# Building the gate tables of a product-key expert layer: bf16 key compares for eight tokens, gates applied by ScalarE

## The chip, the cores and the metric

One core of one Trainium2 chip runs the whole program. The metric is the device time of one execution in microseconds (us). The kernel before takes 3887.56 us, the median of three runs from 3883.04 to 3895.33.

## The reference, cut to what matters

The program is one decoder block on 1024 tokens of 1024 features. Its first part (RWKV-7 time mixing, sparse attention, a merge and a LayerNorm) is not touched here. The change lies in the last part, a layer of 128 x 128 single-neuron experts that are chosen by two keys of 128 values each:

```
s = einsum('thcd,hcnd->thcn', (h @ w_pq) as (token, 8 heads, 2 halves, 64), sub_keys)
s1, i1 = top_k(s[:, :, 0], 16);  s2, i2 = top_k(s[:, :, 1], 16)
top_s, pos = top_k(all sums s1 + s2, 16)           # per token and head
experts = i1 * 128 + i2 at pos                     # 8 heads * 16 = 128 slots per token
gates   = softmax(top_s)
act = gelu(sum_d h[t, d] * u[experts]) * gates;    y[t] = sum over slots act * v[experts]
```

## The kernel before, in words

The 1024 tokens are eight tiles of 128. Tiles 0 to 2 are served by gathering: for each of their 768 rows of experts, GpSimd issues an indirect DMA (L1375) that fetches 128 rows of u or v, and VectorE multiplies and sums them (L1379 for u, L1383 for v). Tiles 3 to 7 (640 tokens) are served densely: all 16384 experts are multiplied with all 640 tokens on TensorE, and a table of gates, zero for an expert that a token did not choose, masks the result. That table `gtD`, token by i1 by i2, is what the change is about.

`retrieve` (one tile) finds the keys: TensorE scores them (L1131), VectorE takes the best sixteen (L1140 to L1148, four steps of two heads each), forms the sums and turns positions into keys and gates (L1154 to L1220). `by_slot` transposes a tile's i1, i2 and gates so that the 128 slots lie on the partitions and the 128 tokens along the free axis (`slots`). `gate_table` then makes the tile's table in 16 blocks of 8 tokens. For each token it needs two matrices of 128 slots x 128 keys: a one-hot matrix of i2 (all eight tokens in one VectorE instruction, L1251), and a one-hot matrix of i1 whose ones are replaced by the slot's gate. The second is made per token: for six tokens of the eight (`ONE_HOT`) by VectorE in fp32, for the other two by a pair of ScalarE instructions:

```
V.tensor_scalar(oh[:, 8 + t], iotan, slots[:, 0, c], slots[:, 2, c], op0=OP.is_equal, op1=OP.mult)   # L1256
A.activation(oh[:, 8 + t], iota, AF.Square, bias=slots[:, 0, c])                                      # L1258
A.activation(oh[:, 8 + t], oh[:, 8 + t], AF.Relu, scale=ng[:, c], bias=slots[:, 2, c])                # L1259
```

TensorE multiplies the two (L1263, one fp32 product per token, which the trace shows as two matmul records), four tokens to a bank of PSUM `tp`, and ScalarE copies each bank (the helper `copy`, L233) into `st`, where the token is the innermost index. Every four blocks `st` goes to `gtD` by DMA (L1267). `gt` has two buffers, `tp` two banks, `st` two halves.

The tables run in a stage of their own, together with other work that the program's scheduler interleaves into one fixed order per engine: 60 of 69 `dots` (a product of a 128-expert slice of u with all 640 tokens: a 512 KB load, ScalarE's split `whi` at L233, GpSimd's `wlo` at L1276, 48 matmuls at L1289 to L1293, and ScalarE's copy `ds`), some 150 rows of the gather, and the retrieval of the next tile. Four times, a tile's table is followed by the end of the next tile's retrieval; tile 7's table comes last and alone. Then the dense stage begins (L1289 to L1293 on u and v, with the rest of the gather beside it).

Of the kernel before, what the change touches and what calls it, by code (L numbers as in the profile page):

```python
# [28 lines left out]
AB = 12  # L29
LAG = 4  # L30
EARLY = 128
ONE_HOT = 6
M1 = 3
J0 = 4
JF = 0
# [16 lines left out]
TD = NG * 128  # L52
# [151 lines left out]
def body(tc, a, out, dbg=None, ntiles=8, mark=lambda s: None):  # L204
# [4 lines left out]
    base = pool("base")  # L209
# [14 lines left out]
    def ptp(dt=F32):  # L224
        return banks[0].tile([128, 512], dt, name="tp", bufs=2)
# [5 lines left out]
    mm = nc.tensor.matmul  # L231
    V, A, G = nc.vector, nc.scalar, nc.gpsimd
    copy = lambda o, i, **k: A.activation(o, i, AF.Copy, **k)  # L233
# [106 lines left out]
        at, n = RW[name]  # L340
        nc.sync.dma_start(dst, a["rows"][0:1, at:at + n].to_broadcast([parts, n]))

    ident, iota, iotan = (base.tile([128, 128], F32, name=n) for n in ("ident", "iota", "iotan"))
# [12 lines left out]
    def constants():  # L356
# [15 lines left out]
        V.tensor_scalar(iotan, iota, -1.0, None, op0=OP.mult)  # L372

        rowb(gnx.rearrange("p a b -> p (a b)"), "gng", 8)
        V.tensor_tensor(gnx, gnx, spread(), op=OP.mult)
# [859 lines left out]
    def by_slot(found, dst):  # L1235

        i1, i2, gates = found
        tp = ptp()
        for n, src in enumerate((i1, i2, gates)):
            nc.tensor.transpose(tp[:, n * 128:(n + 1) * 128], src, ident)  # L1240
        copy(dst[:, 0, :], tp[:, 0:128], scale=-1.0)
        copy(dst[:, 1:3, :].rearrange("p a b -> p (a b)"), tp[:, 128:384])


    def gate_table(i, slots, sl, du, st):
        ng = sl.tile([128, 128], F32, name="ng")
        V.tensor_scalar(ng, slots[:, 2, :], -1.0, None, op0=OP.mult)
        for b in range(max(0, TD - i * 128) // 8, 16):
            s_ = st[:, b // 4 % 2]
            oh = du.tile([128, 16, 128], F32, name="gt", bufs=2)  # L1250
            V.tensor_tensor(oh[:, 0:8], iota[:, None, :].to_broadcast([128, 8, 128]),  # L1251
                            slots[:, 1, b * 8:b * 8 + 8, None].to_broadcast([128, 8, 128]), op=OP.is_equal)
            for t in range(8):
                c = slice(b * 8 + t, b * 8 + t + 1)
                if t < ONE_HOT:
                    V.tensor_scalar(oh[:, 8 + t], iotan, slots[:, 0, c], slots[:, 2, c], op0=OP.is_equal, op1=OP.mult)  # L1256
                else:
                    A.activation(oh[:, 8 + t], iota, AF.Square, bias=slots[:, 0, c])  # L1258
                    A.activation(oh[:, 8 + t], oh[:, 8 + t], AF.Relu, scale=ng[:, c], bias=slots[:, 2, c])  # L1259
            for u in range(2):  # L1260
                tp = ptp()
# [189 lines left out]
    slots = {}  # L1451
# [151 lines left out]
    with tc.tile_pool(reuse_waits=REUSE, name="du", bufs=1) as du, \  # L1603
# [6 lines left out]
        with tc.tile_pool(reuse_waits=REUSE, name="slots", bufs=1) as sl, \  # L1610
                tc.tile_pool(reuse_waits=REUSE, name="ps2", bufs=2, space=PSUM) as banks[0]:
            st = sl.tile([128, 2, 128, 32], F32, name="st")
            found = {}

            def table(i, f=None):
                if f:
                    by_slots(i, f)
                found[i] = gate_table(i, slots[i], sl, du, st)

            for i in slots:  # L1620
                table(i)
# [72 lines left out]
```

## Time and profile before

| | |
|---|---|
| median of three runs | 3887.56 us |
| the profiled execution, its time / its span | 3895.0 / 3893.1 us |
| TensorE (PE) busy in the span | 3552.1 us, 91% |
| VectorE (DVE) busy | 2761.7 us, 71% |
| ScalarE (ACT) busy | 1611.3 us, 41% |
| GpSimd (POOL) busy | 1989.5 us, 51% |
| the stage of the tables | from 1791 to 2504 us of the span |

The shares are averages over stages with different limits: the stage of the tables is read by itself, in windows of the span, by groups of instructions and in order of time. A busy time of a group is the time covered by its instructions; the mean is of single instructions, which overlap a little where they follow each other. L233 is the one line of all ScalarE copies, so those are told apart by the tiles they read and write. The clock is the share of full speed that TensorE was granted.

### The profile page before, as it was taken

Reading aid. Unit: us, or ns where it says so; the run is one execution under the profiler, and the core shown is the slowest. Engines: PE = TensorE matmul, PEld = TensorE weight load, DVE = VectorE, ACT = ScalarE, POOL = GpSimd, SP = SyncE. Lnnn points to the kernel's source line nnn. Section 1 sums busy time; section 2 is a strip of 40 time slices with the busy share of each in tenths; the row PEclk is TensorE's granted clock in tenths of the full one; section 3 lists DMA queues with packets and bytes.
Section 4 is the critical chain, followed back from the end, with each engine's and each line's share of the span. In section 5 each row is a group of like instructions: output and inputs, shape, how many; then the busy total and the mean of one; then the engine's idle time right before and its main releaser. Section 6 shows DMA issues by size and latency. Waiting matters only on the chain.

```text
span 3893.1 us, 65065 instructions
## 1 busy us (share of the span) xinstructions
PE 3552.1 (91%) x24045; PEld 3174.2 (82%) x24045; DVE 2761.7 (71%) x5983; ACT 1611.3 (41%) x2909; POOL 1989.5 (51%) x1566
## 2 busy tenths in 40 slices
PE   8698999888989999688999888899999999999997
PEld 7476777666677777578888888799999999999996
DVE  7556653848377766959999999666776766666753
ACT  3448953243345443425464554632222322222222
POOL 5242222255455553245445454167676666776765
PEclk9899999889999999789999999999999999999998
DMA  6463323864666666277777777589998998898973
GB/s 228 125 189 96 104 90 113 289 198 156 216 216 221 208 219 198 96 259 262 248 259 240 261 262 270 213 315 328 327 329 323 322 329 323 320 334 315 330 255 114
DMA packets 438170, 924.63 MB, mean 238 GB/s; under 512 B 36596, under 2 KB 198588, under 8 KB 434908
## 3 DMA queue, kind: packets, MB, share of 16 engines
q1 hardware_dynamic: 315132, 502.04, 38.6%
q0 software_dynamic: 122720, 418.43, 30.6%
q8 instruction: 190, 3.11, 0.3%
q14 instruction: 128, 1.05, 0.1%
HBM read 792.64 MB, written 127.68 MB: 236 GB/s over the span
## 4 chain that ended last, share of the span: by engine, by line
PE 41%; DVE 20%; DMA 16%; POOL 9%; issue 8%; ACT 4%; SPq 1%; POOLq 0%; ACTq 0%; DVEq 0%
PE pair L1289 5%; PE pair L1291 5%; PE pair L1293 5%; PE acc L429 4%; PE acc L430 4%; PE acc L431 4%; POOL g L1375 4%; POOL wlo L1276 4%; DMA g<-in_v_dram,gidx 3%; DMA raw<-in_ut_dram 3%; DVE pg L1383 3%; DVE gt L1256 3%; DMA g<-in_u_dram,gidx 3%; DMA raw<-in_vt_dram 2%; DVE g L1379 2%
## 5 line engine op out<-in xcount | busy, mean ns | idle before, releaser
L1276 POOL TENSOR_TENSOR wlo<-raw,whi 128x1024 fp32r<-128x1024 f32 x264 | 640.5, 2427 | 304.7 <-ACT whi L233 299.9
L419 POOL TENSOR_TENSOR wlo<-wraw,whi 128x512 fp32r<-128x512 f32 x280 | 374.0, 1338 | 598.8 <-ACT whi L233 530.5
L1383 DVE SCALAR_TENSOR_TENSOR pg<-g,dots,pg 128x1024 f32<-128x1024 f32 x381 | 488.5, 1282 | 154.1 <-DMA g<-in_v_dram,gidx 140.4
L1375 POOL DMA_INDIRECT g<-in_u_dram,gidx x384 | 403.6, 1051 | 354.7 <-DVE g L1379 208.0
L1375 POOL DMA_INDIRECT g<-in_v_dram,gidx x384 | 384.8, 1002 | 368.6 <-DVE pg L1383 167.4
L233 ACT ACTIVATE whi<-raw 128x1024 fp32r<-128x1024 f32 x264 | 278.6, 1056 | 710.0 <-PE pair L1291 366.4
L1289 PE MATMUL pair<-A,whi 128*128 128x320 f32 (+2 forms) x2048 | 482.4, 312 | 25.8 <-DVE A L1321 20.3
L1289 PE MATMUL pair<-h2T,whi 128*128 128x320 f32 x2048 | 478.8, 314 | 14.0 <-DMA h2T<-h2TD 11.1
L1291 PE MATMUL pair<-h2T,whi 128*128 128x320 f32 x2048 | 481.6, 314 | 3.6 <-DMA h2T<-h2TD 3.6
L1291 PE MATMUL pair<-A,whi 128*128 128x320 f32 (+2 forms) x2048 | 481.5, 311 | 2.2 <-DVE A L1321 1.6
L1293 PE MATMUL pair<-A,wlo 128*128 128x320 f32 (+2 forms) x2048 | 480.2, 311 | 2.5 <-POOL wlo L1276 2.5
L1293 PE MATMUL pair<-h2T,wlo 128*128 128x320 f32 x2048 | 480.2, 314 | 0.3 <-POOL wlo L1276 0.3
L429 PE MATMUL acc<-big,whi 128*128 128x512 f32 x864 | 359.8, 417 | 52.3 <-ACT whi L233 18.2
L1379 DVE SCALAR_TENSOR_TENSOR g<-g,pg 128x1024 f32<-128x1024 f32 x256 | 308.8, 1215 | 118.8 <-DMA g<-in_u_dram,gidx 116.4
L1289 PEld LDWEIGHTS pair<-A,whi 128*128 128x128 f32 x2048 | 348.8, 190 | 28.9 <-issue 20.1
L1289 PEld LDWEIGHTS pair<-h2T,whi 128*128 128x128 f32 x2048 | 348.7, 191 | 15.4 <-issue 11.3
L431 PE MATMUL acc<-big,wlo 128*128 128x512 f32 x864 | 353.7, 410 | 2.8 <-POOL wlo L419 2.5
L430 PE MATMUL acc<-big,whi 128*128 128x512 f32 x864 | 352.0, 407 | 3.7 <-DVE big L455 3.7
L1291 PEld LDWEIGHTS pair<-h2T,whi 128*128 128x128 f32 x2048 | 349.2, 191 | 5.4 <-DMA h2T<-h2TD 3.9
L1291 PEld LDWEIGHTS pair<-A,whi 128*128 128x128 f32 x2048 | 349.2, 190 | 3.8 <-DVE A L1321 2.8
L1293 PEld LDWEIGHTS pair<-A,wlo 128*128 128x128 f32 x2048 | 348.7, 190 | 3.0 <-POOL wlo L1276 3.0
L1293 PEld LDWEIGHTS pair<-h2T,wlo 128*128 128x128 f32 x2048 | 348.2, 191 | 2.0 <-POOL wlo L1276 0.5
(483 smaller groups left out, 6632.6 us busy)
## 6 DMA issues: line engine op xcount, KB each, us to landing
raw<-in_vt_dram SPq DMA_DIRECT2D x136, 512.0 KB
raw<-in_ut_dram SPq DMA_DIRECT2D x128, 512.0 KB
gtD<-st SPq DMA_DIRECT2D x20, 2048.0 KB
gt<-gtD SPq DMA_DIRECT2D x32, 1280.0 KB
wraw<-in_wz_dram SPq DMA_DIRECT2D x152, 256.0 KB
dotD<-ds SPq DMA_DIRECT2D x69, 320.0 KB
al<-dotD SPq DMA_DIRECT2D x69, 320.0 KB
mw<-in_wada_dram SPq DMA_DIRECT2D x32, 512.0 KB
```

Source lines behind the costliest of these rows:

```text
L233: copy = lambda o, i, **k: A.activation(o, i, AF.Copy, **k)
L419: G.tensor_tensor(lo, raw, hi.bitcast(F32), op=OP.subtract)
L429: mm(pt, lhsT=wh[:, ks], rhs=ah[:, k, :], start=k == 0, stop=False)
L430: mm(pt, lhsT=wh[:, ks], rhs=al[:, k, :], start=False, stop=False)
L431: ins = mm(pt, lhsT=wl[:, ks], rhs=ah[:, k, :], start=False, stop=k == nk - 1)
L1276: G.tensor_tensor(lo, raw, hi.bitcast(F32), op=OP.subtract)
L1289: mm(pts[n], lhsT=wh, rhs=ah[:, h], start=k == 0, stop=False)
L1291: mm(pts[n], lhsT=wh, rhs=al[:, h], start=False, stop=False)
L1293: mm(pts[n], lhsT=wl, rhs=ah[:, h], start=False, stop=last)
L1375: G.indirect_dma_start(out=u, out_offset=None, in_=a["u" if n < 2 else "v"], in_offset=bass.IndirectOffsetOnAxis(ap=idx[:, k:k + 1], axis=0))
L1379: V.scalar_tensor_tensor(u, u, 1.0, h2, op0=OP.mult, op1=OP.mult, accum_out=dots[:, k:k + 1])
L1383: V.scalar_tensor_tensor(acc, u, dots[:, k:k + 1], acc, op0=OP.mult, op1=OP.add)
```

## The change

`by_slot` now writes i1 as bf16 (128 keys are exact in it) into the third plane of `slots`, and no longer negated. A new constant `keys8` holds each key eight times in a row in bf16, made once by a ScalarE copy. For a block of 8 tokens, one VectorE instruction compares `keys8` with the block's eight first keys and writes a bf16 one-hot `hot`, slot by key by token. Eight ScalarE copies then take token t's column out of it, read with a step of eight elements, and put the gate in as the scale of the copy. So L1256, L1258, L1259 and the constants `iotan` and `ng` go. TensorE's products are the same, but are written to PSUM with the token innermost, so that neighbouring results of one product lie four words apart; ScalarE's copy to `st` then reads PSUM in order and writes runs of four tokens. `gt` grows from 16 to 20 units of 128 words, which is the room that the dense stage's `gt` has anyway.

```diff
-        for n, src in enumerate((i1, i2, gates)):
+        for n, src in enumerate((i2, gates, i1)):
             nc.tensor.transpose(tp[:, n * 128:(n + 1) * 128], src, ident)
-        copy(dst[:, 0, :], tp[:, 0:128], scale=-1.0)
-        copy(dst[:, 1:3, :].rearrange("p a b -> p (a b)"), tp[:, 128:384])
+        copy(dst[:, 0:2, :].rearrange("p a b -> p (a b)"), tp[:, 0:256])
+        copy(first_keys(dst), tp[:, 256:384])
+    first_keys = lambda slots: slots[:, 2, 0:64].bitcast(BF)
...
+            room = du.tile([128, 20, 128], F32, name="gt", bufs=2)
+            oh2, oh1 = room[:, 0:8], room[:, 8:16]
+            hot = room[:, 16:20].rearrange("p a b -> p (a b)").bitcast(BF).rearrange("p (a b) -> p a b", b=8)
+            V.tensor_tensor(hot, keys8, k1[:, None, b * 8:b * 8 + 8].to_broadcast([128, 128, 8]), op=OP.is_equal)
...
             for t in range(8):
-                c = slice(b * 8 + t, b * 8 + t + 1)
-                if t < ONE_HOT:
-                    V.tensor_scalar(oh[:, 8 + t], iotan, slots[:, 0, c], slots[:, 2, c], op0=OP.is_equal, op1=OP.mult)
-                else:
-                    A.activation(oh[:, 8 + t], iota, AF.Square, bias=slots[:, 0, c])
-                    A.activation(oh[:, 8 + t], oh[:, 8 + t], AF.Relu, scale=ng[:, c], bias=slots[:, 2, c])
+                copy(oh1[:, t], hot[:, :, t], scale=slots[:, 1, b * 8 + t:b * 8 + t + 1])
...
-                    mm(tp[:, t * 128:(t + 1) * 128], lhsT=oh[:, 4 * u + t], rhs=oh[:, 8 + 4 * u + t], start=True, stop=True)
+                    mm(tp[:, :, t], lhsT=oh2[:, 4 * u + t], rhs=oh1[:, 4 * u + t], start=True, stop=True)
...
-                copy(s_[:, :, t0:t0 + 4].rearrange("p a b -> p b a"), tp.rearrange("p (b a) -> p b a", b=4))
+                copy(s_[:, :, t0:t0 + 4], tp)
...
+            keys8 = sl.tile([128, 128, 8], BF, name="keys8")
+            copy(keys8, iota[:, :, None].to_broadcast([128, 128, 8]))
```

The scheduler makes a new order for the stage; before it and after it every engine's order is what it was. VectorE near the start of tile 4's table, before (L1383 are rows of the gather, L1140 the next tile's sort):

```order
L1251 TENSOR_TENSOR gt<-iota,slots 128x1024
L1256 TENSOR_SCALAR gt<-iotan,slots 128x128 x6
L1383 SCALAR_TENSOR_TENSOR pg<-g,dots,pg 128x1024
L1251 TENSOR_TENSOR gt<-iota,slots 128x1024
L1256 TENSOR_SCALAR gt<-iotan,slots 128x128 x6
L1383 SCALAR_TENSOR_TENSOR pg<-g,dots,pg 128x1024
L1140 MAX v_16603<-sc 128x8 x4
```

The same place now (L1254 is the bf16 compare, L1255 the compare of second keys, L1138 the sort):

```order
L1254 TENSOR_TENSOR gt<-keys_15601,slots 128x1024
L1255 TENSOR_TENSOR gt<-iota,slots 128x1024
L1383 SCALAR_TENSOR_TENSOR pg<-g,dots,pg 128x1024 x3
L1254 TENSOR_TENSOR gt<-keys_15601,slots 128x1024
L1255 TENSOR_TENSOR gt<-iota,slots 128x1024
L1383 SCALAR_TENSOR_TENSOR pg<-g,dots,pg 128x1024 x2
L1138 MAX v_16580<-sc 128x8 x2
```

Seven instructions per block have become two, and two or three rows of the gather stand between blocks where one stood. Over the four tables that have other work beside them, rows of the gather between a table's first and last block go from 78 to 106 (all in all some 150 stand in the stage in both), all four steps of the next tile's sort stand inside the table where one of them stood behind it, and on TensorE 38.8 `dots` are issued inside those tables where 30.8 were (21.6 between the tables, where 29.5 were).

ScalarE in the last table, before and then now (L233 and L232 are the helper `copy`):

```order
L1258 ACTIVATE gt<-iota,slots 128x128 x2
L1259 ACTIVATE gt<-gt,slots,ng 128x128 x2
L233 ACTIVATE st<-tp 128x4x128 x2
L1258 ACTIVATE gt<-iota,slots 128x128 x2
L1259 ACTIVATE gt<-gt,slots,ng 128x128 x2
```

```order
L232 ACTIVATE gt<-gt,slots 128x128 x8
L232 ACTIVATE st<-tp 128x128x4 x2
L232 ACTIVATE gt<-gt,slots 128x128 x8
L232 ACTIVATE st<-tp 128x128x4 x2
L232 ACTIVATE gt<-gt,slots 128x128 x8
```

Four small instructions per block have become eight, and the two copies out of PSUM walk it in another order. No dot and no row of the gather stands beside the last table, before or now.

## Rows read from the trace of the kernel before

**Rows 1.** Windows: the first four tables, the last table, most of the dense stage.
```profile
core 0: us, PE busy (x) PEld busy (x) DVE busy (x) ACT busy (x) POOL busy (x), PEclk, DMA share, GB/s
1791.00:2451.00 660.00, 594.25 (x4081) 577.06 (x4080) 646.78 (x1637) 341.63 (x568) 318.22 (x208) 0.96 0.75 257
2451.00:2504.00 53.00, 36.69 (x257) 33.70 (x257) 45.76 (x112) 50.13 (x94) 3.26 (x1) 0.90 0.33 136
2600.00:3700.00 1100.00, 1078.47 (x7282) 1074.79 (x7281) 765.26 (x937) 301.09 (x368) 758.34 (x569) 0.99 0.90 325
```

**Rows 2.** Waits between 1791 and 2451: who waited, total, times, longest (us).
```profile
ACT st L233 <- PE tp L1263: 116.1, 52, 8.4
POOL g L1375 <- DVE pg L1383: 85.7, 42, 5.0
...
PE tp L1263 <- DVE gt L1256: 35.1, 19, 3.9
```

**Rows 3.** Groups of VectorE's instructions between 1791 and 2451: busy us, mean ns, idle.
```profile
L1256 DVE TENSOR_SCALAR gt<-iotan,slots 128x128 f32<-128x128 f32 x384 | 162.5, 488 | 0.0
L1383 DVE SCALAR_TENSOR_TENSOR pg<-g,dots,pg 128x1024 f32<-128x1024 f32 x105 | 133.9, 1275 | 6.0 <-DMA g<-in_v_dram,gidx 5.8
L1251 DVE TENSOR_TENSOR gt<-iota,slots 128x1024 f32<-128x1024 f32 x65 | 86.0, 1323 | 0.0
...
L1146 DVE FIND_INDEX8 i<-v,sc 128x8 uint32<-128x128 f32 x64 | 17.9, 280 | 0.0
```

**Rows 4.** All engines in order of time in the last table: one block.
```profile
2466.19 1.95 ACT L233 ACTIVATE st<-tp 128x512 f32<-128x512 f32 x2
...
2467.29 2.07 PE L1263 MATMUL tp<-gt 128*128 128x128 f32 x16 [1.00 <-ACT st L233]
2467.53 1.62 DVE L1256 TENSOR_SCALAR gt<-iotan,slots 128x128 f32<-128x128 f32 x6
2467.92 0.67 ACT L1258 ACTIVATE gt<-iota,slots 128x128 f32<-128x128 f32 x2
...
2468.47 0.87 ACT L1259 ACTIVATE gt<-gt,slots,ng 128x128 f32<-128x128 f32 x2
2469.24 1.95 ACT L233 ACTIVATE st<-tp 128x512 f32<-128x512 f32 x2
```

**Rows 5.** VectorE, then GpSimd, in order of time in tile 4's table: start, length.
```profile
1957.64 3.71 DVE L1256 TENSOR_SCALAR gt<-iotan,slots 128x128 f32<-128x128 f32 x6
...
1956.69 3.30 POOL L1276 TENSOR_TENSOR wlo<-raw,whi 128x1024 fp32r<-128x1024 f32 x1 [0.83 <-ACT whi L233]
```

**Rows 6.** Single lines: instructions, duration in ns as min/median/max, first and last start.
```profile
L1188 DVE TENSOR_TENSOR ge<-wx,ranks x32: 626/692/1233, 918.6 to 2438.8; 128x1024 bf16<-128x1024 bf16 x32
...
L1251 DVE TENSOR_TENSOR gt<-iota,slots x80: 1192/1210/3242, 1791.0 to 2496.9; 128x1024 f32<-128x1024 f32 x80
...
L1196 DVE TENSOR_TENSOR wp<-wp x24: 405/424/2784, 1909.8 to 2442.3; 128x512 bf16<-128x512 bf16 x24
```

**Rows 7.** Windows, sums: the four tables with other work, then the four stretches between.
```profile
sum 403.00, PE 369.49 PEld 355.37 DVE 397.36 ACT 258.33 POOL 181.01; mean PE 92.37 PEld 88.84 DVE 99.34 ACT 64.58 POOL 45.25
...
sum 254.00, PE 222.76 PEld 219.69 DVE 246.42 ACT 82.27 POOL 135.78; mean PE 55.69 PEld 54.92 DVE 61.61 ACT 20.57 POOL 33.94
```

**Rows 8.** Groups of ScalarE's instructions by shape, whole span.
```profile
L233 ACT ACTIVATE st<-tp 128x512 f32<-128x512 f32 x160 | 165.5, 1110 | 119.2 <-PE tp L1263 118.8
...
L1258 ACT ACTIVATE gt<-iota,slots 128x128 f32<-128x128 f32 x160 | 52.6, 386 | 0.0
...
L233 ACT ACTIVATE pT<-tp 128x512 f32<-128x512 f32 x48 | 28.4, 593 | 24.6 <-PE tp L975 24.4
...
L233 ACT ACTIVATE p<-p,asm 128x128 f32<-128x128 f32 x8 | 3.2, 398 | 0.0
```

**Rows 9.** The chain that ended last, pieces in order of time: a block's products; a gather.
```profile
2020.95 1.78 PE tp L1263 x16
...
2139.17 9.79 DMA g<-in_v_dram,gidx
```

More of the change, by code (lines that the diff above doesn't have):

```diff
@@ L31 @@
 EARLY = 128
-ONE_HOT = 6
 M1 = 3
@@ L341, in rowb @@
         nc.sync.dma_start(dst, a["rows"][0:1, at:at + n].to_broadcast([parts, n]))
-    ident, iota, iotan = (base.tile([128, 128], F32, name=n) for n in ("ident", "iota", "iotan"))
+    ident, iota = (base.tile([128, 128], F32, name=n) for n in ("ident", "iota"))
     ranks = base.tile([128, 3, 16], BF, name="ranks")
@@ L371, in constants @@
         nc.sync.dma_start(iota, a["more"][:, 1152:1280])
-        V.tensor_scalar(iotan, iota, -1.0, None, op0=OP.mult)
         rowb(gnx.rearrange("p a b -> p (a b)"), "gng", 8)
@@ L1238, in by_slot @@
         tp = ptp()
-        for n, src in enumerate((i1, i2, gates)):
+        for n, src in enumerate((i2, gates, i1)):
             nc.tensor.transpose(tp[:, n * 128:(n + 1) * 128], src, ident)
-        copy(dst[:, 0, :], tp[:, 0:128], scale=-1.0)
-        copy(dst[:, 1:3, :].rearrange("p a b -> p (a b)"), tp[:, 128:384])
[L1245 to L1248, printed above, removed]
-            s_ = st[:, b // 4 % 2]
-            oh = du.tile([128, 16, 128], F32, name="gt", bufs=2)
-            V.tensor_tensor(oh[:, 0:8], iota[:, None, :].to_broadcast([128, 8, 128]),
-                            slots[:, 1, b * 8:b * 8 + 8, None].to_broadcast([128, 8, 128]), op=OP.is_equal)
-            for t in range(8):
-                c = slice(b * 8 + t, b * 8 + t + 1)
-                if t < ONE_HOT:
-                    V.tensor_scalar(oh[:, 8 + t], iotan, slots[:, 0, c], slots[:, 2, c], op0=OP.is_equal, op1=OP.mult)
-                else:
-                    A.activation(oh[:, 8 + t], iota, AF.Square, bias=slots[:, 0, c])
-                    A.activation(oh[:, 8 + t], oh[:, 8 + t], AF.Relu, scale=ng[:, c], bias=slots[:, 2, c])
@@ new lines, in by_slot, with gate_table @@
+        copy(dst[:, 0:2, :].rearrange("p a b -> p (a b)"), tp[:, 0:256])
+        copy(first_keys(dst), tp[:, 256:384])
+    first_keys = lambda slots: slots[:, 2, 0:64].bitcast(BF)
+    def gate_table(i, slots, sl, du, st, keys8):
+        k1 = first_keys(slots)
+        for b in range(16):
+            s_ = st[:, b // 4 % 2]
+            room = du.tile([128, 20, 128], F32, name="gt", bufs=2)
+            oh2, oh1 = room[:, 0:8], room[:, 8:16]
+            hot = room[:, 16:20].rearrange("p a b -> p (a b)").bitcast(BF).rearrange("p (a b) -> p a b", b=8)
+            V.tensor_tensor(hot, keys8, k1[:, None, b * 8:b * 8 + 8].to_broadcast([128, 128, 8]), op=OP.is_equal)
+            V.tensor_tensor(oh2, iota[:, None, :].to_broadcast([128, 8, 128]),
+                            slots[:, 0, b * 8:b * 8 + 8, None].to_broadcast([128, 8, 128]), op=OP.is_equal)
+            for t in range(8):
+                copy(oh1[:, t], hot[:, :, t], scale=slots[:, 1, b * 8 + t:b * 8 + t + 1])
@@ L1260, in gate_table @@
             for u in range(2):
-                tp = ptp()
+                tp = ptp().rearrange("p (a b) -> p a b", b=4)
                 for t in range(4):
-                    mm(tp[:, t * 128:(t + 1) * 128], lhsT=oh[:, 4 * u + t], rhs=oh[:, 8 + 4 * u + t], start=True, stop=True)
+                    mm(tp[:, :, t], lhsT=oh2[:, 4 * u + t], rhs=oh1[:, 4 * u + t], start=True, stop=True)
                 t0 = b % 4 * 8 + 4 * u
-                copy(s_[:, :, t0:t0 + 4].rearrange("p a b -> p b a"), tp.rearrange("p (b a) -> p b a", b=4))
+                copy(s_[:, :, t0:t0 + 4], tp)
@@ L1617, in table @@
                     by_slots(i, f)
-                found[i] = gate_table(i, slots[i], sl, du, st)
+                found[i] = gate_table(i, slots[i], sl, du, st, keys8)
             for i in slots:
```

## The prediction

> **What bounds the kernel now.** I read the windows of the stage first, then who waits for whom, then the costliest groups on the fullest engine, and last the order of time in one block. The change touches nothing outside 1791 to 2504 us, so only this stage is priced. In its first 660 us VectorE is busy 646.8 us, 98%, and TensorE 594.3 us, 90%; in the dense stage behind it TensorE is at 1078.5 of 1100 us, 98%, and VectorE has room [rows 1]. So VectorE sets the pace of the first four tables. The waits agree: GpSimd's gathers wait for VectorE to free a buffer, and TensorE's products for the gates that VectorE writes; what ScalarE waits for most is those products [rows 2]. The group that costs VectorE most is L1256, the six fp32 instructions per block that this change removes: 162.5 us [rows 3].
>
> Part of that is not work. Six of them take 1.62 us undisturbed [rows 4], so the 64 blocks hold 64 x 1.62 = 104 us of work; the other 59 us are spent as where the six take 3.71 us while GpSimd's `wlo` runs [rows 5].
>
> In the last table (2451 to 2504 us) the pace is another engine's: ScalarE is busy 50.1 of 53 us [rows 1]. It takes 2469.24 - 2466.19 = 3.05 us per block, and TensorE waits 1 us per block for its copy out of PSUM [rows 4]. Here a faster VectorE buys nothing, and any time added on ScalarE is paid in full.
>
> **VectorE's part.** Out go L1256's 162.5 us. In come 64 bf16 compares of 128x1024. The nearest row is L1188, the same compare of a bf16 tile of that size with a short row repeated along it: 0.69 us [rows 6], so 64 x 0.69 = 44 us. They can meet `wlo` too: L1251 beside them pays 1323 - 1210 = 0.11 us for it on the mean [rows 3, 6], which makes 51 us, and L1196, a bf16 instruction, has met it for up to 2.8 us [rows 6]. The bounds are thus 51 us and 44 + 59 = 103 us (all of L1256's waiting stays); VectorE sheds 111 us or 60 us. I take 111, since half of the instructions that could wait are gone. L1251 itself is unchanged.
>
> **What the stage then takes.** VectorE falls from 647 to 536 us (587 at worst), below TensorE's 594. TensorE's work is the same, so it becomes the limit, but not everywhere, because the new order moves work. A dot is 48 matmuls at 1078.5 / 7282 = 0.148 us [rows 1], 7.1 us. Eight dots more inside the tables, eight fewer between:
> - tables: TensorE 369.5 + 57 = 426 us; VectorE 397.4 + 28 gather rows x 1.28 [rows 3] + four sort steps of twenty instructions at 0.28 (22) - 111 = 344 us [rows 7] (395 at worst);
> - between: TensorE 222.8 - 57 = 166 us; VectorE 246.4 - 27 x 1.28 - 22 = 190 us.
>
> The longer ones are 426 + 190 = 616 us; at the dense stage's 98% that is 628 us. [...] I take 620: **-40 us** (bounds: 603 with no loss, -57; 646 if TensorE reaches 94% in the tables, -14). What is late next is then a product of TensorE's, and VectorE begins to wait for `gt` buffers.
>
> **ScalarE's part.** Per block the four small instructions (0.67 + 0.87 us [rows 4], less overlap) become eight copies with a scale per partition. The row is `p<-p,asm`, such a copy of 128x128: 398 ns alone [rows 8]. Two L1258 of 386 ns take 0.67, so in a run each hides 0.10 us: 0.30 us per copy, 2.4 us for eight. No row shows what it costs to read every eighth element. The upper bound is the copy `st<-tp`, which writes with a long step: 1110 ns against 593 for `pT<-tp`, the same 512 elements written in order [rows 8], 1.0 ns more per element, 0.13 per copy: 0.43, 3.4 us for eight. The two copies to `st` now write four words in a row; between 0.49 us each (as `pT`, less overlap) and today's 0.95. The block is thus 3.4 to 5.3 us. I take 3.75 (0.33 and 0.55): the row with a price has its step on the write, and that step has become runs of four. For the last table: 16 x (3.75 - 3.05) = **+11 us** (bounds +6 and +36). In the first four tables ScalarE has the cover: it is busy 258 of 403 us [rows 7].
>
> [...]
>
> **At nothing:** `keys8` is one ScalarE copy ahead of the first table, while VectorE is still at the retrieval; `by_slot` keeps two copies, `ng` and `iotan` are two small VectorE instructions. SP issues the same loads and stores, GpSimd the same gathers and `wlo`; the same bytes in 620 us are a DMA share of 0.75 x 660 / 620 = 0.80, and the dense stage runs at 0.90 [rows 1]. If that cover failed, a gather that arrives late costs up to 9.8 us at a time on the chain [rows 9].
>
> **Sum:** -40 + 11 = -29 us on the profiled execution's 3895.0: 3866. That execution is 7.4 us above the median of 3887.56, so on the median I predict **3858**. The dense stage's order is the same, and it starts when the last table is written, so the gain is kept.
>
> **Rivals.**
> *A, slower: the products' new place in PSUM.* Each product now writes results four words apart. No row shows a matmul that does so. If it costs what a stepped write costs ScalarE, a factor 1110 / 593 = 1.87 [rows 8], a block's products rise from 1.78 [rows 9] by 1.55 us; 64 blocks add 99 us to TensorE in the tables: (426 + 99 + 190) / 0.98 = 730, +70, and with the last table's +11 the time is 3887.6 + 81 = 3969. It decides from about 0.45 us per block (25%), where the 29 us are used up. Against it: a product needs 1.78 / 8 = 0.22 us for 128 results per partition, 1.7 ns each, while the dots write one in 0.148 / 320 = 0.46 ns, so the write side has room. 18%. [...]
> *B: ScalarE becomes the limit.* At 5.3 us per block it needs 85 us a table, and some 20 for the dots and scores, 105 of TensorE's 106. An engine that works in order and waits for products will not fill that: 115 us a table, 460 + 194 = 654, -6, and +36 at the end: 3918. For it, ScalarE's many waits for products [rows 2]; against it, that needs both upper bounds at once. 8%.
> *C: the time does not come free.* Both engines are now loaded alike and tied by two buffers; TensorE has 92% of the table windows today [rows 7]. At 94% the first four tables give -14, with the last table's +11 that is -3: 3885. 17%.
>
> **Chances.** The forecast with its neighbours (3830 to 3875) has 57%. A measurement of this kernel can tell about 0.3%, 12 us, from no change. Faster takes the forecast and a little of C: 0.60; same most of C and the mild ends of A and B: 0.17; slower the rest of A and B: 0.23. The range reaches from the gain with no loss (-57 + 6, 3836, and a few us for the clock, 3830) to B's end, 3918; most of A lies outside. The forecast's own range is 3830 to 3875.
>
> **What the profile after would show.** Right: the compare near 0.7 us, TensorE above 94% and VectorE under 92% between 1791 and the last table, that stretch near 620 us, the last table near 64 us with ScalarE full. A shows as products of a block over 2.2 us, B as ScalarE copies over 0.4 us and ScalarE over 90% in the tables, C as waits of TensorE for ScalarE's or VectorE's `gt` that replace those for L1256. Wrong altogether if the first four tables stay at 660 us although L1256 is gone.

## The result, and the profile after

The changed kernel takes 3912.65 us (median of 20 runs, 3893.93 to 3922.2) against 3887.62 us of the kernel before (20 runs): a ratio of 1.0059, 95% interval 1.0047 to 1.0071. It is slower by 25 us; the prediction was 3858, faster. The profiled execution took 3913.4 us, with a span of 3911.6 against 3893.1 before.

The windows of the changed kernel: the first four tables (1787 to 2439), the last (2439 to 2514), most of the dense stage.

```profile
1787.00:2439.00 652.00, 593.91 (x4073) 578.43 (x4073) 533.08 (x1314) 408.06 (x826) 311.48 (x210) 0.95 0.75 261
2439.00:2514.00 75.00, 47.11 (x286) 43.33 (x285) 29.11 (x32) 70.31 (x163) 2.35 (x1) 0.80 0.23 97
2600.00:3700.00 1100.00, 1072.48 (x7227) 1069.62 (x7226) 762.68 (x941) 301.46 (x369) 753.43 (x566) 0.99 0.90 324
```

Against [rows 1], VectorE's share in the first four tables fell from 98% to 533.08 / 652 = 82%, but TensorE's only rose from 90% to 91%: no engine fills the stretch any more, and the stretch is hardly shorter. Measured from the first table's first compare of second keys to the last table's first, the four take 651.9 us against 659.8, and the last, from there to the start of its last eviction (ScalarE's copy out of a bank of PSUM into `st`), 74.2 against 52.1. These two measures, "four" and "last", stand in the table below for every run. The stage is 14 us longer in the profiled execution. The rest of the span's 18.5 us lies behind it (1398.4 us from the stage's end on, against 1390.2) and ahead (it starts 4 us earlier). In the profiled executions that follow the part behind lies between 1384.6 and 1411.6 us without an order that fits the edits, so I do not read a cause into it.

The groups of VectorE and TensorE between 1787 and 2439, then of ScalarE over the whole span:

```profile
L1255 DVE TENSOR_TENSOR gt<-iota,slots 128x1024 f32<-128x1024 f32 x65 | 83.8, 1289 | 1.4 <-ACT slots L232 1.4
L1254 DVE TENSOR_TENSOR gt<-keys,slots 128x1024 bf16<-128x1024 bf16 x64 | 55.8, 877 | 16.5 <-PE tp L1263 7.7 <-ACT gt L232 7.2 <-issue 1.6
L1263 PE MATMUL tp<-gt 128*128 128x128 f32 x1024 | 131.6, 283 | 21.8 <-ACT st L232 12.4 <-ACT sc L232 4.8 <-DVE pos L1173 3.3
```

```profile
L232 ACT ACTIVATE gt<-gt,slots 128x128 f32<-128x128 bf16 x640 | 273.6, 514 | 82.3 <-DVE gt L1254 73.6 <-issue 3.9 <-DVE v L1142 3.4
...
L232 ACT ACTIVATE st<-tp 128x512 f32<-128x512 f32 x160 | 87.3, 584 | 42.7 <-PE tp L1263 41.5 <-issue 1.2
```

L1256's 162.5 us [rows 3] became 55.8 us of the bf16 compare: VectorE sheds 107 us there. The evictions `st<-tp`, which now write runs of four words, fell from 1110 [rows 8] to 584 ns (e1, where this layout is the only edit, has 597). But ScalarE has 640 scaled copies, 273.6 us, where L1258 took 52.6 us [rows 8] and L1259 another 70.3: over the whole stage it gains 151 us and sheds 78.

The waits between 1787 and 2439:

```profile
POOL wlo L1276 <- ACT whi L232: 101.0, 35, 11.1
...
ACT gt L232 <- DVE gt L1254: 71.9, 23, 7.6
...
DVE pg L1383 <- DMA g<-in_v_dram,gidx: 42.4, 22, 5.1
ACT st L232 <- PE tp L1263: 38.7, 28, 5.5
```

ScalarE waited 116.1 us for products before [rows 2] and 38.7 now: it comes late more often, and it waits itself, 71.9 us for VectorE's compares. GpSimd's `wlo` waits 101.0 us for ScalarE's `whi` (37.2 before), and VectorE, early now, waits for gathered rows. TensorE's own waits for ScalarE in the same stretch:

```profile
PE tp L1263 <- ACT st L232: 12.4, 7, 5.5
PE tp L1129 <- ACT st L232: 7.5, 6, 4.7
PE pair L1289 <- ACT ds L232: 5.6, 3, 3.0
PE tp L1263 <- ACT sc L232: 4.8, 3, 3.1
```

These are 30 us. Before, TensorE waited 35.1 us there for L1256 [rows 2] and 1.8 us for ScalarE: one late engine has replaced the other. Pieces of the chain that ended last show whom the stage waits for (the copies `gt` are 13.9% of it between 1787 and 2600, more than any other line); before, L1256 led there, and products and gathers stood among the pieces [rows 9]:

```profile
1981.44 3.41 ACT gt L232 x8
1985.82 3.33 ACT gt L232 x8
1991.64 3.30 ACT gt L232 x8
```

One block of the last table, all engines in order of time, against [rows 4]:

```profile
2461.83 1.06 ACT L232 ACTIVATE st<-tp 128x512 f32<-128x512 f32 x2
...
2462.47 2.05 PE L1263 MATMUL tp<-gt 128*128 128x128 f32 x16 [2.21 <-ACT st L232]
2462.78 3.40 ACT L232 ACTIVATE gt<-gt,slots 128x128 f32<-128x128 bf16 x8
...
2464.96 0.69 DVE L1254 TENSOR_TENSOR gt<-keys,slots 128x1024 bf16<-128x1024 bf16 x1 [2.79 <-issue]
2465.57 1.22 DVE L1255 TENSOR_TENSOR gt<-iota,slots 128x1024 f32<-128x1024 f32 x1
2466.09 1.06 ACT L232 ACTIVATE st<-tp 128x512 f32<-128x512 f32 x2
```

ScalarE has no gap: 3.40 us for eight copies, then two evictions; 2466.09 - 2461.83 = 4.26 us per block where it was 3.05. TensorE's idle time per block rose from 1.0 to 2.21 us; its products themselves are as long as before (2.05 against 2.07 us).

### The profile page after: what moved, and what is told of

It is laid out like the page before. It is cut to its first block, busy times and chain, and to the rows that moved or that the text cites. A ratio compares the mean times of both kernels' runs of the same rounds, so it can differ in the third digit from the quotient of the medians.

```text
span 3911.6 us, 64943 instructions
## 1 busy us (share of the span) xinstructions
PE 3558.2 (91%) x24044; PEld 3184.5 (81%) x24045; DVE 2626.4 (67%) x5577; ACT 1695.5 (43%) x3230; POOL 1981.0 (51%) x1566
## 4 chain that ended last, share of the span: by engine, by line
PE 47%; DVE 17%; DMA 15%; ACT 8%; issue 7%; POOL 6%; SPq 0%; POOLq 0%; ACTq 0%; DVEq 0%
PE pair L1289 7%; PE pair L1291 7%; PE pair L1293 7%; PE acc L427 4%; PE acc L428 4%; PE acc L429 4%; DMA g<-in_v_dram,gidx 4%; DMA g<-in_u_dram,gidx 3%; ACT gt L232 3%; POOL g L1375 3%; DMA raw<-in_ut_dram 2%; POOL wlo L1276 2%; DVE pg L1383 2%; DVE g L1379 2%; PE acc L979 1%
## 5 line engine op out<-in xcount | busy, mean ns | idle before, releaser
L1383 DVE SCALAR_TENSOR_TENSOR pg<-g,dots,pg 128x1024 f32<-128x1024 f32 x381 | 489.6, 1285 | 179.5 <-DMA g<-in_v_dram,gidx 175.9
L232 ACT ACTIVATE whi<-raw 128x1024 fp32r<-128x1024 f32 x264 | 278.7, 1056 | 662.2 <-PE pair L1291 304.8
```

The source lines that it names most:

```text
L1383: V.scalar_tensor_tensor(acc, u, dots[:, k:k + 1], acc, op0=OP.mult, op1=OP.add)
```

## The experiments

**Theory S:** ScalarE's load is what the change lost by: eight copies per block stand in its order ahead of the evictions that free TensorE's banks, and this takes back what VectorE's relief is worth. **Theory T**, the rival: TensorE was so near its limit in the first four tables that no relief there is worth much. The stepped write into PSUM (rival A of the prediction) was tried along with them. Medians of a ratio's two sides are from runs on one chip; "four" and "last" are from one profiled execution each.

| run | median us | ratio to before (95%) | four | last |
|---|---|---|---|---|
| before | 3887.62 | 1 | 659.8 | 52.1 |
| the change | 3912.65 | 1.0059 (1.0047 to 1.0071) | 651.9 | 74.2 |
| e1, products alone | 3889.61 | 0.999 (0.997 to 1.001) | 658.7 | 45.9 |
| e2, keys alone | 3934.28 | 1.0104 (1.0059 to 1.0149) | 659.9 | 84.6 |
| e3, `hot` by token | 3889.72 | 1.0004 (0.9982 to 1.0025) | 652.3 | 56.0 |
| e4, two copies | 3825.75 | 0.9821 (0.9774 to 0.9869) | 575.0 | 72.7 |
| e5, VectorE's relief alone | 3840.35 | 0.9869 (0.9824 to 0.9913) | 588.2 | 70 |
| e6, the same and products | 3844.98 | 0.989 (0.9849 to 0.9931) | 596.7 | 69.2 |
| e7, bf16 products | 3993.16 | 1.027 (1.0227 to 1.0312) | 736.8 | 73 |
| e8, gates by VectorE | 3965.94 | 1.0178 (1.0147 to 1.021) | 717.6 | 62.1 |
| e9, gates halved | 3895.16 | 1.0019 (1.0002 to 1.0035) | 667.8 | 48.7 |
| e10, bf16, written in a row | 4037.59 | 1.0371 (1.0346 to 1.0396) | 768.9 | 79.5 |
| e11, copies ahead | 3909.88 | 1.0054 (1.0035 to 1.0074) | 652.4 | 70.9 |
| e12, four and four | 3869.26 | 0.9924 (0.99 to 0.9948) | 644.2 | 46.3 |
| e13, two and six | 3877.18 | 0.9955 (0.9938 to 0.9971) | 634.2 | 61.7 |

Every run has its own order from the scheduler, which moves some dots too. In e4, e5 and e6 about 265 matmuls of dots stand beside the last table that stood in the four before, and in e13 81; at the 0.148 us per matmul of [rows 1] that is 39 and 12 us of TensorE's work. Where it matters, the sum of "four" and "last" is the fairer measure.

**e1, the kernel before with the products' new layout alone.**

```diff
-                tp = ptp()
+                tp = ptp().rearrange("p (a b) -> p a b", b=4)
-                    mm(tp[:, t * 128:(t + 1) * 128], lhsT=oh[:, 4 * u + t], ...
+                    mm(tp[:, :, t], lhsT=oh[:, 4 * u + t], ...
-                copy(s_[:, :, t0:t0 + 4].rearrange("p a b -> p b a"), tp.rearrange("p (b a) -> p b a", b=4))
+                copy(s_[:, :, t0:t0 + 4], tp)
```

> The kernel before with one part of the change alone: products written with tokens innermost, ScalarE's copy to st reads PSUM in order. Theory S (ScalarE's load is what the change lost by): the copy falls from 1.10 to about 0.58 us, products stay at 0.275 us per record, the last table falls from 53 us to VectorE's pace of about 2.8 us per block (45 us), the first four tables stay VectorE's: 3880 us, 6 to 10 below before. Theory T (TensorE was near its limit in the tables, so nothing there is worth much): the last table the same, 3880 us. If the stepped PSUM write costs TensorE anything, records over 0.30 us and a time at or above before.

Measured: no change, 0.999. Its products and evictions as single lines (instructions, ns as min/median/max):

```profile
L1263 PE MATMUL tp<-gt x1280: 270/275/582, 1787.6 to 2489.6; 128*128 128x128 f32 x183
```
```profile
L233 ACT ACTIVATE st<-tp x160: 575/597/601, 1790.9 to 2489.9; 128x512 f32<-128x512 f32 x160
```

The products keep their 275 ns, and the evictions are cheaper by half a microsecond each. That is worth 6 us in the last table, where ScalarE sets the pace, and 1 us in the four, where VectorE does, in the profiled execution; the interval of the medians is too wide to show so little. Rival A falls.

**e2, the other part alone:** the change with the lines of e1's diff put back as they were before.

> The change without its products part: bf16 keys and eight ScalarE copies per block, but products one behind the other in PSUM and the old copy to st. Theory S: ScalarE pays 2 x 0.5 us more per block, 5.3 us in all: last table 75 + 16 = 91 us, and the first four tables, where ScalarE already holds TensorE up, longer by another 15 to 30 us: 3940 to 3960 us. Theory T: only the last table grows, 3928 us.

Measured: 1.0104. The longer evictions (1096 ns at the median) come on top of the copies: 8 us more in the four tables and 10 in the last than in the change. ScalarE's 128 evictions in the four tables are 128 x (1101 - 585) ns = 66 us longer in all (means), so about an eighth of that shows; in the last table it is 10 of 17 us. The four tables lie between the theories (15 to 30 us by S, none by T): a microsecond of ScalarE's has no fixed price there.

**e3, the compare writes `hot` by token,** so that each copy reads 128 elements in a row.

```diff
-            hot = ....rearrange("p (a b) -> p a b", b=8)
-            V.tensor_tensor(hot, keys8, k1[:, None, b * 8:b * 8 + 8].to_broadcast([128, 128, 8]), op=OP.is_equal)
+            hot = ....rearrange("p (a b) -> p a b", a=8)
+            V.tensor_tensor(hot, keys8[:, None, :].to_broadcast([128, 8, 128]),
+                            k1[:, b * 8:b * 8 + 8, None].to_broadcast([128, 8, 128]), op=OP.is_equal)
-                copy(oh1[:, t], hot[:, :, t], ...
+                copy(oh1[:, t], hot[:, t], ...
```

> The change with hot laid out by token, so that each ScalarE copy reads 128 neighbouring bf16 values in place of every eighth; VectorE's compare then has a repeated value innermost. Theory S: copies fall from 0.51 to 0.40 us, 0.11 less in a run, a block 0.9 us less on ScalarE: last table 75 to 61 us, first four tables 5 to 15 us shorter although VectorE's compare goes from 0.69 to 1.2 us: 3885 to 3893 us. Theory T: last table 61 us, the rest as in the change or longer by VectorE's 64 x 0.5 us: 3899 to 3920 us.

Measured: 1.0004, 23 us below the change. The copies as a single line, of the change and then of e3:

```profile
L232 ACT ACTIVATE gt<-gt,slots x640: 501/511/556, 1790.2 to 2508.4; 128x128 f32<-128x128 bf16 x160
```
```profile
L232 ACT ACTIVATE gt<-gt,slots x640: 384/390/483, 1792.1 to 2494.1; 128x128 f32<-128x128 bf16 x160
```

Reading every eighth element costs 511 - 390 = 121 ns per copy. The compare pays for the layout instead: its mean went from 877 ns in the change (first four tables) to 1567 in e3 (from 1787 to 2400 us). The last table, ScalarE's, falls from 74.2 to 56.0. The four stay, where theory S had 5 to 15 us less; I read that as one engine's gain against the other's loss, which no run separates.

**e4, the change with two copies per block in place of eight;** the products of the other six tokens use the matrices of these two, so six gates of eight are left out.

```diff
-            for t in range(8):
+            for t in (0, 4):
...
-                    mm(tp[:, :, t], lhsT=oh2[:, 4 * u + t], rhs=oh1[:, 4 * u + t], ...
+                    mm(tp[:, :, t], lhsT=oh2[:, 4 * u + t], rhs=oh1[:, 4 * u], ...
```

> The change with two of the eight ScalarE copies per block (tokens 0 and 4; the other six products read those two matrices, so six of eight tokens get a neighbour's gates). Everything else as in the change. Theory S: with ScalarE's 6 x 0.41 us per block gone, TensorE paces: first four tables 652 to about 615 us, last table 75 to about 40 us: 3840 to 3850 us. Theory T: the last table falls to 40 us, but the first four stay above 640: 3870 to 3880 us.

Measured: 0.9821. The windows of its first four tables and its last:

```profile
1787.00:2362.00 575.00, 537.83 (x3809) 525.33 (x3807) 526.67 (x1313) 247.20 (x430) 301.30 (x204) 0.97 0.82 286
2362.00:2435.00 73.00, 72.54 (x546) 72.55 (x547) 34.43 (x34) 43.11 (x77) 14.59 (x6) 0.98 0.44 165
```

Six copies less per block take 77 us off the four tables and 78 off the stage. About half of the 77 are the 39 us of dots that now stand beside the last table, which is why that one is not near the 40 us of both theories. TensorE is now busy 537.83 of 575 us, 94%, and 72.54 of 73 in the last; its waits for ScalarE in the four tables fall from 30 to 9 us. Theory T had the four above 640 us; with the 39 us put back they are at 614. Theory T falls, and S holds in that the copies are what costs.

**e5, the kernel before with VectorE relieved as the change relieves it,** and ScalarE's work as before: L1256 goes, one bf16 compare whose result is not used comes in, and six products of eight take a matrix that ScalarE wrote (six gates are left out).

```diff
-            for t in range(8):
+            V.tensor_tensor(hot, keys8, keys8[:, 0:1, :].to_broadcast([128, 128, 8]), op=OP.is_equal)
+            for t in range(ONE_HOT, 8):
...
-                    mm(..., rhs=oh[:, 8 + 4 * u + t], ...
+                    mm(..., rhs=oh[:, 14 + u], ...
```

> The kernel before with VectorE relieved as in the change and ScalarE loaded as before: L1256 goes, one bf16 compare per block comes (its result is not used), and the six products of those tokens read the matrices that ScalarE makes for the other two (so six of eight tokens get a neighbour's gates). Theory S (VectorE's relief is worth what was forecast, ScalarE's copies took it back): first four tables 580 to 625 us in place of 660, last table about 53 us as before: 3815 to 3850 us. Theory T (relieving VectorE is worth little because TensorE stands at its limit): first four tables 645 us or more, 3873 us or more.

**e6, e5 with e1's products.**

> As the run with VectorE relieved and ScalarE as before, and the products written with tokens innermost as well, so ScalarE's two copies out of PSUM per block take 0.58 in place of 1.10 us. Six of eight tokens get a neighbour's gates. Theory S: ScalarE's time counts in both stretches once VectorE is relieved: another 10 to 25 us off, 3800 to 3830 us. Theory T: only the last table gains, 8 to 16 us.

Measured: 0.9869 and 0.989. The windows of e5:

```profile
1797.00:2385.00 588.00, 542.98 (x3810) 529.40 (x3809) 530.12 (x1315) 330.23 (x557) 302.59 (x203) 0.97 0.80 279
2385.00:2455.00 70.00, 67.91 (x524) 67.61 (x522) 35.13 (x31) 59.13 (x105) 15.17 (x7) 1.00 0.46 166
```

With ScalarE at 330 of 588 us, as before, VectorE's relief brings the stage from 712 to 658 us. This is the prediction's first term by itself: it is there, 54 us of the stage in the profiled execution where 40 were forecast, and 34 to 68 us off the median by the interval. The last table is at 70 us and not near 53, since dots stand beside it. TensorE waits 3.6 us for ScalarE in the four tables. Theory S gave e6 another 10 to 25 us, and that failed: ScalarE's cheaper evictions add nothing that can be told from e5 (the intervals overlap, and the stage is 666 us against 658). Where TensorE hardly waits for ScalarE, less time on ScalarE bought nothing.

**e7, both one-hot matrices in bf16,** the gate as two bf16 parts that VectorE multiplies in, two bf16 products per token, no scaled copies.

```diff
+            V.tensor_tensor(h2, keys8, of(keys, 0), op=OP.is_equal)
+            V.tensor_tensor(h1, keys8, of(keys, 1), op=OP.is_equal)
+            V.tensor_tensor(gh, h1, of(parts, 0), op=OP.mult)
+            V.tensor_tensor(gl, h1, of(parts, 1), op=OP.mult)
...
+                    mm(tp[:, :, e], lhsT=h2[:, :, e], rhs=gh[:, :, e], start=True, stop=False)
+                    mm(tp[:, :, e], lhsT=h2[:, :, e], rhs=gl[:, :, e], start=False, stop=True)
```

> A version meant to keep VectorE's relief without ScalarE's copies: both one-hots made by bf16 compares of eight tokens, the gate split into two bf16 parts that are multiplied in by two more VectorE instructions, and two bf16 products per token (one per part, summed in PSUM) in place of one in fp32; ScalarE only copies PSUM out. Theory S: ScalarE falls to 1.1 us per block, VectorE takes 4 x 0.7 = 2.8 us per block plus waits for GpSimd (3.75 us before with waits): first four tables 610 to 630 us, last table about 45 us, 3835 to 3855 us; TensorE's products cost under 0.1 us per record if the stepped reads are free. Theory T: VectorE's load is nearly that of before, so 3870 to 3885 us.

**e10, e7 with each product written in a row into PSUM,** and the evictions of before.

```diff
-                    mm(tp[:, :, t], ...
+                    mm(tp[:, t * 128:(t + 1) * 128], ...
```

> The kernel with the bf16 products (both one-hot matrices and the two bf16 parts of the gate), with each product's results written in a row into PSUM as before the change, and the long-step copy out of PSUM of before (about 1.1 us). Its matrices are still read with a step of 16 bytes. If the stepped write into PSUM is what made the bf16 products take 0.235 us for 128 columns, they fall to 0.06 to 0.12 us, TensorE loses up to 100 us in the four tables, and VectorE sets the pace at about 2.8 us per block: four tables near 610 us or less, 3840 to 3870 us. If it is the stepped read of the moving matrix, the products stay at 0.23 us each and the time near 3990, with the longer copies out of PSUM on top.

Measured: 1.027 and 1.0371. TensorE's products of e7 in order of time, and then e10's as groups of the first four tables:

```profile
2530.39 0.41 PE L1265 MATMUL tp<-gt 128*128 128x128 bf16 x1
...
2530.62 0.42 PE L1266 MATMUL tp<-gt 128*128 128x128 bf16 x1
...
2530.86 0.42 PE L1265 MATMUL tp<-gt 128*128 128x128 bf16 x1
```
```profile
L1265 PE MATMUL tp<-gt 128*128 128x128 bf16 x436 | 177.8, 415 | 0.5 <-DVE gt L1258 0.5
L1266 PE MATMUL tp<-gt 128*128 128x128 bf16 x435 | 176.6, 414 | 0.0
```

One product of e7 starts every 0.235 us for 128 columns, and the record is as long whether PSUM is written with a step (e7) or in a row (e10): 415 ns. So it is not the write. What both runs share is that the two matrices are read with a step of 16 bytes. Products of this size and type whose matrices are read in a row stand in the first part of the kernel before, here three of them:

```profile
595.34 0.34 PE L935 MATMUL tp<-pre_b,gh 128*128 128x128 bf16 x3
```

The three take 0.34 us together; with that line's shortest record, 219 ns, they start about (0.34 - 0.22) / 2 = 0.06 us apart, an estimate. This fits the step as the cause and does not show it: no run changed the step alone, nor one of the two reads. Both theories had reckoned with under 0.1 us per product, which e7 and e10 do not have, so these runs decide nothing between them.

**e8, the gates put in by one VectorE multiplication,** and **e9, four tokens by it and four by copies** (its diff has 4 for 8, and keeps the copies of tokens 4 to 7).

```diff
-            for t in range(8):
-                copy(oh1[:, t], hot[:, :, t], scale=slots[:, 1, b * 8 + t:b * 8 + t + 1])
+            V.tensor_tensor(oh1[:, 0:8], hot[:, :, 0:8].rearrange("p a t -> p t a"),
+                            slots[:, 1, b * 8:b * 8 + 8, None].to_broadcast([128, 8, 128]), op=OP.mult)
```

> The changed kernel with its eight ScalarE copies per block replaced by one VectorE multiplication of the bf16 matrix by the gates (128x1024, written by token in fp32). VectorE should pay about what the other fp32 instruction of this size takes, 1.21 us, so 3.1 us per block in place of 1.9; ScalarE keeps only its evictions, about 1.06 us per block. Theory S (ScalarE's copies are what the change lost by): VectorE becomes the limit again but less than before, tables 374 + 77 = 452 us and between 159, 611 in all, four tables near 625 us, last table about 52: near 3865 us. Theory T (TensorE was near its limit, so VectorE's and ScalarE's loads are worth little): four tables stay near 645 to 650, 3890 us.

> The changed kernel with the gates of four tokens of a block put in by one VectorE multiplication (128x512) and those of the other four by ScalarE's scaled copies. VectorE pays some 0.6 us per block more than in the changed kernel (2.5), ScalarE some 1.8 us less (4 x 0.43 + 1.06 = 2.8, less than the 3.05 of before). Theory S: four tables near 605 to 615 us with TensorE the limit, last table near 50, so near 3850 us, faster than both kernels. Theory T: no better than the run with all gates by VectorE, near 3890.

Measured: 1.0178 and 1.0019. Both are far above what theory S gave, and e8 is above theory T's figure too. The multiplication as a single line, of e8:

```profile
L1257 DVE TENSOR_TENSOR gt<-gt,slots x80: 1926/1997/4635, 1801.6 to 2573.6; 128x1024 f32<-128x1024 bf16 x80
```

It takes 2.00 us, not 1.21, and the one of e9, for four tokens, 1.07 where 0.6 was expected. The step of its read may be the reason, but the operation and the type of the input differ from the compare's as well, and no run separates them. So a block costs VectorE 3.9 us in e8, and the four tables take 717.6 us. Both theories had the same wrong term here; e8 says only that VectorE's load counts as well.

**e11, meant to change the order alone:** the compares and copies of block b + 1 ahead of the products and evictions of block b.

```diff
+        ready = gates(0)
         for b in range(16):
+            (oh2, oh1), ready = ready, gates(b + 1) if b < 15 else None
```

> The changed kernel with the compares and scaled copies of block b+1 put ahead of the products and evictions of block b; the work is the same. If it is ScalarE's order that costs (it waits for products while TensorE waits for copies), the waits of ScalarE for TensorE's products and of TensorE for ScalarE's evictions shrink in the first four tables and they fall by 20 us or more, near 3890 us. If it is ScalarE's load, the last table stays near 74 us and the four tables move by less than 10 us: within 0.3% of the changed kernel's 3912.65.

Measured: 1.0054, the change's own time. ScalarE in its last table, in order of time:

```profile
2473.59 1.06 ACT L232 ACTIVATE st<-tp 128x512 f32<-128x512 f32 x2
...
2474.54 3.42 ACT L232 ACTIVATE gt<-gt,slots 128x128 f32<-128x128 bf16 x8
2477.84 1.08 ACT L232 ACTIVATE st<-tp 128x512 f32<-128x512 f32 x2
```

A block still takes 2477.84 - 2473.59 = 4.25 us. But the edit hardly moved anything on ScalarE. In the change's own order the copies of block b + 1 already stand ahead of block b's evictions: so it is for 149 of the 160 evictions there, and for 150 in e11. So e11 tried no other order, and does not separate ScalarE's load from the place of its copies. In the last table ScalarE has no gap, and there its load is the price. In the four tables the change's trace shows the place at work, here in order of time:

```profile
2198.95 1.95 PE L1263 MATMUL tp<-gt 128*128 128x128 f32 x16
...
2201.00 3.42 DVE L1254 TENSOR_TENSOR gt<-keys,slots 128x1024 bf16<-128x1024 bf16 x1
...
2204.52 3.40 ACT L232 ACTIVATE gt<-gt,slots 128x128 f32<-128x128 bf16 x8 [5.87 <-DVE gt L1254]
...
2207.83 1.05 ACT L232 ACTIVATE st<-tp 128x512 f32<-128x512 f32 x2
...
2208.45 1.91 PE L1263 MATMUL tp<-gt 128*128 128x128 f32 x12 [3.75 <-ACT st L232]
```

The products end at 2200.90, and their banks could be emptied from then on. ScalarE waits until 2204.52 for a late compare, makes the next block's eight copies, and evicts at 2207.83; TensorE has stood idle 3.75 us when its next products start. All nine waits of TensorE for `st` in the four tables that are over 0.5 us have such eight copies just ahead of the eviction. An order with the evictions ahead of them was not tried.

**e12 and e13, a complete kernel with fewer copies:** the compare and the copies for four (six) tokens of eight, the fp32 instruction of before for the others. The lines are e12's.

```diff
+            for t in range(4):
+                V.tensor_scalar(oh1[:, t], iota, slots[:, 2, 64 + b * 4 + t:65 + b * 4 + t],
+                                slots[:, 1, b * 8 + t:b * 8 + t + 1], op0=OP.is_equal, op1=OP.mult)
-            for t in range(8):
-                copy(oh1[:, t], hot[:, :, t], ...
+            for t in range(4, 8):
+                copy(oh1[:, t], hot[:, :, t - 4], ...
```

> The changed kernel with the bf16 compare and the scaled ScalarE copies for four tokens of a block only (the compare is 128x512, about 0.36 us; four copies, about 1.7 us), and the fp32 instruction of before that compares and puts in the gate at once for the other four (4 x 0.27 us on VectorE). Per block, undisturbed: VectorE 0.36 + 1.08 + 1.21 = 2.65 us (2.83 before, 1.9 in the change), ScalarE 1.7 + 1.06 = 2.8 (3.05 before, 4.3 in the change). Theory S: both engines are below before, so the time is below before: the four tables some 10 to 25 us shorter than 660, the last near 50, near 3870 us. Theory T: same as before, 3885 to 3890.

> The same with six tokens by the bf16 compare and ScalarE's copies and two by the fp32 instruction. Per block: VectorE 0.53 + 0.54 + 1.21 = 2.3 us, ScalarE 6 x 0.42 + 1.06 = 3.6. Theory S: the last table is set by ScalarE, 16 x 3.6 = 58 to 62 us; in the first four tables what VectorE gains over the run with four and four is given back by ScalarE, so 635 to 650 and 3875 to 3885 us. If VectorE's load counts for more than ScalarE's there, four tables fall below 630 and it is the faster of the two.

Measured: 0.9924 and 0.9955. e12, which leaves nothing out, is faster than both kernels. Its blocks in the last table, in order of time, and its copies as a single line:

```profile
2453.58 1.11 DVE L1259 TENSOR_SCALAR gt<-iota,slots 128x128 f32<-128x128 f32 x4
2453.78 1.06 ACT L232 ACTIVATE st<-tp 128x512 f32<-128x512 f32 x2
...
2454.41 2.05 PE L1267 MATMUL tp<-gt 128*128 128x128 f32 x16 [0.45 <-ACT st L232]
2454.61 0.41 DVE L1255 TENSOR_TENSOR gt<-keys,slots 128x512 bf16<-128x512 bf16 x1
2454.94 1.22 DVE L1256 TENSOR_TENSOR gt<-iota,slots 128x1024 f32<-128x1024 f32 x1
2455.06 1.32 ACT L232 ACTIVATE gt<-gt,slots 128x128 f32<-128x128 bf16 x4 [0.21 <-DVE gt L1255]
2456.08 1.11 DVE L1259 TENSOR_SCALAR gt<-iota,slots 128x128 f32<-128x128 f32 x4
2456.28 1.06 ACT L232 ACTIVATE st<-tp 128x512 f32<-128x512 f32 x2
```
```profile
L232 ACT ACTIVATE gt<-gt,slots x320: 389/398/422, 1799.1 to 2483.4; 128x128 f32<-128x128 bf16 x160
```

A block takes 2456.28 - 2453.78 = 2.50 us, against 3.05 before and 4.26 in the change, and VectorE (0.41 + 1.22 + 1.11, less overlap) now fills it while ScalarE waits 0.21. e13 gives VectorE still less and has the shorter four tables (634.2; some 12 us of what they are shorter are dots that stand beside the last table instead), but its last table pays six copies (61.7). Both lie in or near what theory S gave.

## Why the prediction was wrong

**The step that failed is ScalarE's part:** "In the first four tables ScalarE has the cover: it is busy 258 of 403 us". I set its added time there at nothing because its average had room. The windows of the tables and of the stretches between, summed as in [rows 7], show where the forecast's 620 us went:

```profile
sum 468.00, PE 439.54 PEld 426.74 DVE 374.27 ACT 340.42 POOL 218.15; mean PE 109.89 PEld 106.69 DVE 93.57 ACT 85.10 POOL 54.54
```
```profile
sum 184.00, PE 154.37 PEld 151.69 DVE 158.81 ACT 67.64 POOL 93.32; mean PE 38.59 PEld 37.92 DVE 39.70 ACT 16.91 POOL 23.33
```

- **Between the tables** the length held, 184 us where 190 were forecast, but in part by luck: VectorE was to fill it with 190 us of work and has 158.81, the rest is idle time.
- **In the tables** about 430 us were forecast (620 less 190, with 426 of TensorE's work) and they took 468. TensorE's own work there is 439.5 us; the rest is idle time, 28 us, at 94%, the share of rival C. An engine that is 340 of 468 us busy, 73%, was not cover, since its 3.4 us of copies per block stand ahead of the evictions that free TensorE's banks (the rows at e11), and TensorE (30 us) and GpSimd (101) wait for it meanwhile. e4 measures the term: six copies of eight less, 64 blocks x 6 x 0.43 = 165 us of ScalarE's time in the four tables, take 78 us off the stage; and e5, with VectorE's relief but without the copies, has a stage of 658 us where the change has 726. How much of this is ScalarE's load and how much the place of the copies stays open.
- **The copy's price** was taken as 0.33 us and is 3.40 / 8 = 0.43 with its overlap, the upper bound; the evictions were taken as 0.55 and are 0.53. The last table's term was +11 and came out at +22, at 4.26 us per block where 3.75 was taken. I had put the row with a price on the write above the read, for which no row stood; e3 shows the read at 511 against 390 ns.

**VectorE's part was right.** The compare is 686 ns where 0.69 us was forecast, and VectorE shed 107 us where I took 111. It is busy 533 us in the first four tables where 536 were forecast; only the split was off (374 in the tables and 159 between, where I had 344 and 190). e5 has this term without ScalarE's: 54 us off the stage, and 1.3% (0.9869, 0.9824 to 0.9913), some 51 us, off the median, an interval that holds the forecast's 40. TensorE is at 542.98 / 588 = 92% in its four tables and not at 98%: there the dots that are left over go beside the last table instead.

**The sum** was -40 + 11 = -29. In the profiled execution the same two terms are -8 and +22, +14; the median's +25 holds some 11 us more. Of these 6.6 come from the two profiled executions, which lie 7.4 us (before) and 0.8 us (after) above their medians; the other 4 lie outside the stage, and their cause stays open. The forecast's 620 us in place of 628, its bound of 603 and the 3830 of its range count on time gained by a higher clock in the tables, a term that no run shows: the granted clock in the first four tables was 0.95 in the change and 0.96 before [rows 1], and 0.97 in e4 and e5, where TensorE is 94% and 92% busy.

**The rivals.** A is refuted for these products: 275 ns in both layouts. B has the cause, ScalarE, at milder prices: its block is 4.26 us and not 5.3, and it gave 3918, with +36 in the last table and -6 in the four; 3912.65 is next to it, in part by luck, since the terms were +22 and -8. Its sign, ScalarE over 90% busy in the tables, did not come either: it is at 73%. I gave it 8% since I asked for both upper bounds at once; the copy's alone was enough. C has TensorE's 94% but not its reason: TensorE waits for evictions and hardly for ScalarE's `gt` (1.3 us). And the sign that I had set for being wrong altogether, the four tables still at 660 us, is nearly met at 651.9.

## What to carry to other kernels

Room in an engine's average (ScalarE, 73% busy in the tables) was no cover here, where the added work stands in its order ahead of what frees another engine's buffers. Such work had no fixed price here (165 us of copies left out took 78 us off the stage, 66 us of longer evictions cost 8 us in the four tables), so measure it by leaving most of it out. Where work moves from one engine to another, a split can beat both ends; here four tokens of eight did (0.9924, 0.99 to 0.9948), eight lost. A layout that made one instruction cheap made its reader pay here (511 against 390 ns), so price a step at every engine that reads it. And before a run is read as a test of an order, see in its trace that the order is another one.

## What the runs showed of the hardware

- ScalarE's scaled copy of 128 bf16 elements takes 390 ns read in a row (e3), 398 with a step of 8 bytes (e12), 456 with 12 (e13) and 511 with 16 (the change). Between 8 and 16 bytes each byte of the step costs about (511 - 398) / 8 = 14 ns per copy, an estimate from these rows; up to 8 bytes the step cost 8 ns in all. So four tokens innermost read nearly as fast as a row. The copies of e13 as a single line:

```profile
L232 ACT ACTIVATE gt<-gt,slots x480: 444/456/495, 1783.9 to 2473.6; 128x128 f32<-128x128 bf16 x160
```

- VectorE's multiplication that reads bf16 at a step of 16 bytes and writes fp32 takes 2.00 us for 128x1024 (e8), where the fp32 compare of that size takes 1.21 [rows 6], (1997 - 1210) / 1024 = 0.8 ns more per element. No run shows whether the step makes it.
- fp32 products that write PSUM four words apart have records of 275 ns (e1), as those that write in a row (275, before), and the copy out of it that then writes runs of four words takes 597 ns (e1) in place of 1110 [rows 8].
- bf16 products whose matrices are read with a 16-byte step start every 0.235 us (e7), more than the 0.22 us of a whole fp32 product (1.78 us for eight [rows 9]), so two bf16 products in place of one fp32 lost TensorE time. Three such products read in a row take 0.34 us together (L935 of the kernel before). No run changed the step alone.
